# Attention weights and gates from sigmoids and a running product, in place of clamp, exp, ln, running sum and exp

## The chip, the cores and the metric

The kernel runs on one core of a Trainium2 chip. The metric is device time in microseconds (us). Three timed runs of the kernel before gave 1094.94, 1096.07 and 1101.93 us, so its time is 1096.07 us (median).

The engines of the core are named as the profile names them. PE is TensorE, which multiplies matrices, and PEld is its loading of weights. DVE is VectorE, ACT is ScalarE, POOL is GpSimd, and SP is SyncE, which issues transfers. Each engine works through its own queue in order and waits on semaphores for the others. Matmul results land in eight PSUM banks, numbered 0 to 7 here. In this kernel DVE and ACT read them, and POOL does not.

## The reference

The kernel is one layer of a streaming encoder over 1024 tokens of width 1024, all in float32. One input projection feeds three groups of heads (stick-breaking attention, an mLSTM matrix memory, a gated MLP). Then come one output projection, a mixture of 32 experts and a gated embedding. Three pieces of it matter here:

```python
# stick-breaking attention, 6 heads of 64, query blocks of 128 (n = 0..7), scale = 1/8
z = jnp.einsum('bthd,bshd->bhts', q[:, t0:kend], k[:, :kend]) * scale
mask = spos[None, :] < tpos[:, None]
log_1m = jnp.where(mask, -jax.nn.softplus(z), 0.0)
after = lax.cumsum(log_1m, axis=3, reverse=True) - log_1m
a = jnp.where(mask, jnp.exp(jax.nn.log_sigmoid(z) + after), 0.0)
outs.append(jnp.einsum('bhts,bshd->bthd', a, v[:, :kend]))
...
# mLSTM inputs: convolved queries and keys, and the log of the forget gate
qk = jax.nn.silu(causal_depthwise_conv(jnp.concatenate([qb, kb], axis=-1), conv_w[i], conv_b[i]))
bcum = jnp.cumsum(jax.nn.log_sigmoid(f_pre.reshape(Bn, N, L, H)), axis=2)
...
yb = hb * jax.nn.sigmoid(ob)
```

The weight of key s for query t is sigmoid(z_s) times the product, over the keys after s, of one minus their sigmoid. The reference forms that product as the exponential of a sum of logs.

## The kernel before, in words

The program has three parts in time. First the input is normed and turned, and the first columns of the input projection are made (up to about 87 us of the span). Then the rest of the input projection and the whole attention run interleaved (about 87 to 460 us). After that come the mLSTM rows, the output projection, routing, experts and the embedding. The change touches the second part alone.

**Steps and slots.** The attention is cut into 48 `Step`s: 6 heads times 8 query blocks, in the order of blocks (0, 7, 1, 6, 2, 5, 3, 4). A step of block i has 128 queries and n = 128 (i + 1) keys, so small and large steps alternate. The order in which every engine gets its work is written out by hand (L1077 to L1120): a loop over 58 slots (`NSLOT + 2`), and in slot s each stage of the pipeline is issued for another step. The second number below is how many slots after its scores a stage of the same step comes.

- `scores` (0): PE makes z into banks 3 and 4, at most 512 columns each, and adds a large negative number over the diagonal block's masked part.
- `clamp` (1): DVE reads z from PSUM, scales it by 1/8, caps it at 40 and writes `zc`. One instruction for each bank, 72 in all.
- `softplus` (1): ACT makes exp of `zc` into `sp`, then ln(1 + sp).
- `sums` (2): DVE makes the running sum of `sp` from the last key to the first, then POOL subtracts it from `zc`.
- `weights` (3): ACT makes exp of that.
- `turned` (4): PE transposes the weights into banks 5 and 6.
- `high` and `low` (5): ACT copies them to float16, and DVE makes the float16 remainder.
- `values` (6): PE multiplies with the values into bank 7, and `finish` (7): DVE adds the two halves into `ya`.

In a slot the queues of DVE, ACT and POOL receive `finish`, `clamp`, `high`, `weights`, `softplus`, `sums`, `low`, and then the side work. PE receives half a projection group, `values`, the rest of the slot's projection work, `turned`, `scores`. The 88 half groups of the projection are spread over 56 slots, so one or two fall into a slot, with shorter matmuls for some groups than for others.

**Side work.** What follows a projection is a generator that moves on by one stage for each slot. `ob_out` makes the output gate sigmoid(ob): DVE scales and caps, ACT does exp, ln(1 + .) and exp(-.), POOL multiplies with a gain. `conv_out` makes the causal convolution of 128 rows by 1024 tokens with four DVE instructions, then the SiLU in the same way: DVE caps (L548), ACT does exp, ln and exp, POOL multiplies. There are 8 `ob` tiles and 6 convolutions. `gate_rows` makes the mLSTM gates from exp and ln and, later, three exps. Other side work is the splitting of the next weights into two float16 parts (ACT L259, DVE L252), the gated MLP (`sgu`) and the splitting of the output weights (L140 and L141).

**Buffers.** `zc` has two buffers for each of two widths (512 and 1024), `sp` has one for each width. The weights for the experts are read into memory that the input projection uses, so their transfers can only be issued when this part is over.

**Activation tables.** ACT evaluates functions from a loaded table set, and a load is an instruction of its own, `ACT_TABLE_LOAD`. Before, the set with both exp and ln is loaded at the start (L149) and again after the one GELU (L480, L481). The experts begin with another (L1800).

Of the kernel before, what the change touches and what calls it, by code (L numbers as in the profile page):

```python
# [10 lines left out]
F32 = mybir.dt.float32  # L11
F16 = mybir.dt.float16
I32 = mybir.dt.int32
AF = mybir.ActivationFunctionType
# [29 lines left out]
ZCLAMP = 40.0  # L44
# [51 lines left out]
def hybrid_kernel(ctx, tc, x, p, norm1_g, w_in, conv_w, conv_b, igate_b, fgate_b, mnorm_g, sb_out_g,  # L96
# [52 lines left out]
    nc.scalar.preload_act_table_set("natural_log_exp_and_others")  # L149
# [28 lines left out]
    # DRAM scratch  # L178
# [12 lines left out]
    # one arena whose slices are first the operands of the input projection, then expert weights  # L191
# [13 lines left out]
    class Slots:  # L205
        """Slices of the arena in turn, by tag."""
# [15 lines left out]
    # matmuls whose results nothing reads: they keep the clock of the tensor engine up while it waits  # L222
# [72 lines left out]
    V = vp.tile([P, NT, HA, 2, DA], F16, name="V")  # L295

# [135 lines left out]
    # work that follows a projection moves on by one stage per slot  # L432
# [43 lines left out]
    def uv_out(pz, a, t):  # L476
        nc.scalar.activation(uv[:, t, a], pz[:, :WU], AF.Copy, scale=ISW)
        yield
        if a and t == NT - 1:
            nc.scalar.activation(uv, uv, AF.Gelu_apprx_tanh)  # L480
            nc.scalar.preload_act_table_set("natural_log_exp_and_others")  # L481
            side.append(sgu_all())
# [16 lines left out]
    def ob_out(pz, t):  # L499
        zr = wp.tile([P, HM * (DM + 1)], F32, "zr")[:, :WM]  # L500
        nc.vector.tensor_scalar(gates[:, :, t], pz[:, WM:WM + 8].rearrange("p (q h) -> p q h", q=2), ISW, None, op0=OP.mult)
        nc.vector.tensor_scalar(zr, pz[:, :WM], -ISW, ZCLAMP, op0=OP.mult, op1=OP.min)
        yield
        nc.scalar.activation(zr, zr, AF.Exp)
        nc.scalar.activation(zr, zr, AF.Ln, bias=one1)
        nc.scalar.activation(zr, zr, AF.Exp, scale=-1.0)
# [24 lines left out]
    def conv_out(pz, jj, half):  # L531
# [16 lines left out]
        nc.vector.tensor_scalar(sg, ca, -1.0, ZCLAMP, op0=OP.mult, op1=OP.min)  # L548
        yield
        nc.scalar.activation(sg, sg, AF.Exp)  # L550
        nc.scalar.activation(sg, sg, AF.Ln, bias=one1)
        nc.scalar.activation(sg, sg, AF.Exp, scale=-1.0)
# [10 lines left out]
    # gate rows: partition = (chunk of P tokens, head), column = token of the chunk  # L563
    def gate_rows():
# [18 lines left out]
        yield  # L583
        nc.scalar.activation(ga, ga, AF.Exp)
# [37 lines left out]
    # output projection weights, over what the attention no longer needs  # L622
# [13 lines left out]
    class Step:  # L636
# [18 lines left out]
        def clamp(self):  # L655
            self.w = 512 if self.n <= 512 else S
            self.zc = at.tile([P, self.w], F32, name=f"zc{self.h}{self.i}", tag=f"zc{self.w}")
            for s0, m, pz in self.z:
                nc.vector.tensor_scalar(self.zc[:, s0:s0 + m], pz[:, :m], 0.125, ZCLAMP, op0=OP.mult, op1=OP.min)  # L659

        def softplus(self):
            self.sp = at.tile([P, self.w], F32, name=f"sp{self.h}{self.i}", tag=f"sp{self.w}", bufs=1)
            nc.scalar.activation(self.sp[:, :self.n], self.zc[:, :self.n], AF.Exp)  # L663
            nc.scalar.activation(self.sp[:, :self.n], self.sp[:, :self.n], AF.Ln, bias=one1)

        def sums(self):
            n, sp = self.n, self.sp[:, :self.n]
            nc.vector.tensor_tensor_scan(sp[:, ::-1], one1.to_broadcast([P, n]), sp[:, ::-1],  # L668
                                         0.0, op0=OP.mult, op1=OP.add)
            nc.gpsimd.tensor_tensor(self.zc[:, :n], self.zc[:, :n], sp, op=OP.subtract)  # L670

        def weights(self):
            nc.scalar.activation(self.zc[:, :self.n], self.zc[:, :self.n], AF.Exp)

        def turned(self):
            h, i = self.h, self.i
            self.t = []
            for s0 in range(0, i + 1, 4):
                m = min(4, i + 1 - s0)
                pt = bank("56", f"at{h}{i}{s0}")  # L680
                for b in range(m):
                    nc.tensor.transpose(pt[:, b * P:(b + 1) * P], self.zc[:, (s0 + b) * P:(s0 + b + 1) * P], ident)
                self.t.append((m, pt))

        def high(self):
            self.a = []
            for s, (m, pt) in enumerate(self.t):
                ah = at.tile([P, 512], F16, name=f"ah{self.h}{self.i}{s}", tag="ah", bufs=3)
                nc.scalar.activation(ah[:, :m * P], pt[:, :m * P], AF.Copy)
                self.a.append(ah)  # L690

        def low(self):
            for s, (m, pt) in enumerate(self.t):
                al = at.tile([P, 512], F16, name=f"al{self.h}{self.i}{s}", tag="al", bufs=3)
                nc.vector.tensor_tensor(al[:, :m * P], pt[:, :m * P], self.a[s][:, :m * P], op=OP.subtract)
                self.a[s] = [(self.a[s][:, b * P:(b + 1) * P], al[:, b * P:(b + 1) * P]) for b in range(m)]

        def values(self):
            self.pa = bank("7", f"av{self.h}{self.i}")[:, :P].rearrange("p (l d) -> p l d", l=2)
            for sb, (ah, al) in enumerate(sum(self.a, [])):  # L700
# [21 lines left out]
    class Rows:  # L722
        """mLSTM chunk, output projection, second norm and routing of P tokens."""
# [165 lines left out]
        # the last tile goes to the router without the way over its rows in memory  # L889
# [97 lines left out]
        def slots(self, which="4"):  # L987
# [8 lines left out]
            # the tokens of the first two experts are also found without the way through memory  # L996
# [68 lines left out]
    with tc.manual_schedule(engines=FOUR):  # L1065
# [11 lines left out]
        for s in range(NSLOT + 2):  # L1077
# [24 lines left out]
            stage(s - 7, "finish")  # L1102
            stage(s - 1, "clamp")
            stage(s - 5, "high")
            stage(s - 3, "weights")
            stage(s - 1, "softplus")
            stage(s - 2, "sums")
            stage(s - 5, "low")
# [5 lines left out]
            stage(s - 6, "values")  # L1114
# [3 lines left out]
            stage(s - 4, "turned")  # L1118
# [29 lines left out]
    # the slot table: (token, row of h2 to add to, weight)  # L1148
# [27 lines left out]
    # LE[., t, e]: whether token t needs no expert after e  # L1176
# [760 lines left out]
```

## Time and profile before

| what | value |
|---|---|
| time, median of 3 runs | 1096.07 us (1094.94 to 1101.93) |
| span of the profiled execution | 1098.5 us |
| PE busy | 948.8 us (86%) |
| DVE busy | 785.3 us (71%) |
| ACT busy | 626.7 us (57%) |
| POOL busy | 433.0 us (39%) |

For the profiled execution the page lists its span and no other time, so its span is taken as its time; it lies inside the range of the timed runs. Shares are means over the whole span, and the three parts of the program have different limits, so the second part is best read by stretches. A row of the view by stretches gives the stretch, its length, and for each engine its busy microseconds with the number of instructions, then the granted PE clock (1.00 is full) and the share of the transfer engines. A row of a group of instructions gives line, engine, operation, what is written from what, shapes and count, then the busy time, the mean nanoseconds of one, and the idle time of the engine just before them with what ended it. In a timeline the idle time before an instruction stands in square brackets.

### The profile page before, as it was taken

To read this page: it belongs to the slowest core of one execution; us is meant where nothing else is said; L and a number is where in the kernel's file an instruction comes from. 1 tells how busy PE (TensorE), PEld (TensorE's weight loads), DVE (VectorE), ACT (ScalarE), POOL (GpSimd) and SP (SyncE) were. 2 spreads that over 40 slices of the span, in tenths; PEclk is the share of its full clock that TensorE was granted. 3 is DMA by queue.
4 is the path that set the end of the run, shared out by engine and by line. 5 is a ranking of instruction groups with operands and counts; after the bars stand their busy time and mean duration, and the time that the engine had idled before them with its cause. 6 is when DMAs were issued, how large, how long until landed. Compare 5 with 4: busy or idle time off the path is not lost. (4 is left out here: it accounts for less than half of the span.)

```text
span 1098.5 us, 16018 instructions
## 1 busy us (share of the span) xinstructions
PE 948.8 (86%) x5927; PEld 546.8 (50%) x5928; DVE 785.3 (71%) x1345; ACT 626.7 (57%) x960; POOL 433.0 (39%) x381
## 2 busy tenths in 40 slices
PE   7899988877899887899788569998899989999796
PEld 4458845444465454665554334444454544544343
DVE  4444659998896997657888747898668686776333
ACT  4335565555587665423343247898667777686422
POOL 2101215454344244322323636854346445552421
PEclk8999989999899988899998689999899999999998
DMA  6421112021221127885348688999979898997330
GB/s 213 124 50 28 36 48 53 20 68 60 70 90 37 35 76 235 254 264 173 102 135 269 207 272 266 318 305 309 301 248 309 259 327 280 291 316 254 76 87 38
DMA packets 128466, 189.55 MB, mean 173 GB/s; under 512 B 13505, under 2 KB 104223, under 8 KB 128384
## 3 DMA queue, kind: packets, MB, share of 16 engines
q1 hardware_dynamic: 113376, 154.40, 43.6%
q0 software_dynamic: 14864, 33.57, 11.2%
q8 instruction: 47, 0.77, 0.3%
q10 hardware_dynamic: 144, 0.52, 0.1%
q14 instruction: 35, 0.29, 0.1%
HBM read 166.01 MB, written 37.31 MB: 185 GB/s over the span
## 5 line engine op out<-in xcount | busy, mean ns | idle before, releaser
L670 POOL TENSOR_TENSOR zc<-zc,sp 128x128 f32<-128x128 f32 (+7 forms) x48 | 71.6, 1491 | 192.8 <-DVE sp L668 174.4
L1277 POOL DMA_INDIRECT h2s<-yo,tabs x32 | 75.7, 2366 | 75.7 <-issue 24.6
L144 PE MATMUL pg<-arena,xT 128*128 128x512 f16 x256 | 97.6, 381 | 0.9 <-ACT xT L1239 0.7
L145 PE MATMUL pg<-arena,xT 128*128 128x512 f16 x256 | 97.8, 382 | 0.0
L146 PE MATMUL pg<-arena,xT 128*128 128x512 f16 x256 | 97.8, 382 | 0.0
L141 DVE SCALAR_TENSOR_TENSOR arena<-arena 128x2048 f16<-128x2048 f32 (+1 forms) x39 | 80.9, 2088 | 22.6 <-ACT arena L140 22.6
L146 PEld LDWEIGHTS <-arena 128*128 128x128 f16 x516 | 52.3, 101 | 53.0 <-issue 12.0
L141 DVE SCALAR_TENSOR_TENSOR arena<-ws,arena 128x2048 f16<-128x2048 f32 x29 | 65.9, 2288 | 14.3 <-ACT arena L140 14.3
L144 PEld LDWEIGHTS <-arena 128*128 128x128 f16 x516 | 53.3, 103 | 38.6 <-issue 7.3
L145 PEld LDWEIGHTS <-arena 128*128 128x128 f16 x516 | 52.4, 102 | 38.7 <-issue 11.4
L140 ACT ACTIVATE arena<-arena 128x2048 f16<-128x2048 f32 (+1 forms) x39 | 67.1, 1738 | 3.8 <-DMA arena<-in_w_up_dram 3.8
L668 DVE TENSOR_TENSOR_SCAN sp<-one,sp 128x128 f32<-128x128 f32 (+7 forms) x48 | 68.1, 1418 | 0.3
L663 ACT ACTIVATE sp<-zc 128x128 f32<-128x128 f32 (+7 forms) x48 | 32.7, 681 | 57.7 <-DVE zc L659 57.5
L659 DVE TENSOR_SCALAR zc<-z 128x512 f32<-128x512 f32 (+3 forms) x72 | 37.5, 548 | 28.9 <-PE z L650 17.8
L140 ACT ACTIVATE arena<-ws 128x2048 f16<-128x2048 f32 x29 | 55.1, 1920 | 0.1
L145 PE MATMUL pd<-dl,hT 128*128 128x512 f16 x120 | 47.0, 392 | 5.4 <-DVE dl L141 5.3
L144 PE MATMUL po<-woh,yT 128*128 128x512 f16 x128 | 50.3, 393 | 0.0
L145 PE MATMUL po<-wol,yT 128*128 128x512 f16 x128 | 50.2, 392 | 0.0
L146 PE MATMUL po<-woh,yT 128*128 128x512 f16 x128 | 49.9, 390 | 0.0
L144 PE MATMUL pd<-dh,hT 128*128 128x512 f16 x120 | 47.2, 394 | 1.6 <-ACT yo L1274 1.5
L701 PE MATMUL av<-V,ah 128*128 128x128 f16 x216 | 25.7, 224 | 26.2 <-DVE ya L707 26.0
L141 DVE SCALAR_TENSOR_TENSOR dl<-arena,dh 128x2048 f16<-128x2048 f32 x17 | 38.9, 2288 | 11.7 <-ACT dh L140 11.7
(664 smaller groups left out, 2858.2 us busy)
## 6 DMA issues: line engine op xcount, KB each, us to landing
arena<-in_w_down_dram SPq DMA_DIRECT2D x19, 1024.0 KB, 11.8
arena<-in_w_up_dram SPq DMA_DIRECT2D x18, 1024.0 KB, 12.4
arena<-in_w_gate_dram SPq DMA_DIRECT2D x17, 1024.0 KB, 10.1
ws<-in_w_gate_dram SPq DMA_DIRECT2D x14, 1024.0 KB
ws<-in_w_up_dram SPq DMA_DIRECT2D x13, 1024.0 KB, 10.7
ws<-in_w_down_dram SPq DMA_DIRECT2D x12, 1024.0 KB, 5.6
arena<-in_w_in_dram SPq DMA_DIRECT2D x16, 384.0 KB, 7.2
x<-in_x_dram SPq DMA_DIRECT2D x8, 512.0 KB, 3.4
```

The lines of the kernel that those rows point to most:

```text
L140: nc.scalar.activation(hi, src, AF.Copy, scale=scale)
L141: nc.vector.scalar_tensor_tensor(lo, src, scale, hi, op0=OP.mult, op1=OP.subtract)
L144: nc.tensor.matmul(o, a[0], w[0], start=first, stop=False)
L145: nc.tensor.matmul(o, a[0], w[1], start=False, stop=False)
L146: nc.tensor.matmul(o, a[1], w[0], start=False, stop=last)
L659: nc.vector.tensor_scalar(self.zc[:, s0:s0 + m], pz[:, :m], 0.125, ZCLAMP, op0=OP.mult, op1=OP.min)
L663: nc.scalar.activation(self.sp[:, :self.n], self.zc[:, :self.n], AF.Exp)
L668: nc.vector.tensor_tensor_scan(sp[:, ::-1], one1.to_broadcast([P, n]), sp[:, ::-1], 0.0, op0=OP.mult, op1=OP.add)
L670: nc.gpsimd.tensor_tensor(self.zc[:, :n], self.zc[:, :n], sp, op=OP.subtract)
L701: nc.tensor.matmul(self.pa.rearrange("p l d -> p (l d)"), ah, V[:, sb, self.h].rearrange("p l d -> p (l d)"), start=(sb == 0), stop=False)
L1277: return nc.gpsimd.indirect_dma_start(out=h2s, out_offset=bass.IndirectOffsetOnAxis(ap=self.tb[:, 1:2], axis=0), in_=self.yo, in_offset=No ...
```

## The change: what it does

The weights of the attention are made as sigmoid(z/8) times the running product of sigmoid(-z/8) over the later keys, and the two gates as sigmoids. For the attention:

- `clamp` and `softplus` become `sigmoids` (1 slot after the scores, as before): ACT reads z from PSUM twice, once for sigmoid(-z/8) into `rest` and once for sigmoid(z/8) into `a`. With two banks these are four instructions, with one bank two.
- `sums` becomes `products` (2): DVE makes the running product of `rest` in place from the last key to the first, with the two operations of the scan both multiplications; POOL multiplies `a` with `rest` shifted by one column. A column of ones stands after the last key.
- `weights` is gone, and `turned`, `high`, `low`, `values` and `finish` each come one slot earlier.
- `rest` has one buffer for each width, as `sp` had; `a` has two, as `zc` had.

In `ob_out` one sigmoid of ACT from PSUM replaces DVE's capping and three ACT instructions, and the POOL multiplication comes one slot earlier. In `conv_out` one sigmoid replaces DVE's capping and three ACT instructions. The table set with the sigmoid is loaded at the start and after the GELU. `gate_rows` still needs exp and ln and loads the set with both in the middle of the attention; a function that the loaded set lacks gets a load in front of it.

```diff
-    nc.scalar.preload_act_table_set("natural_log_exp_and_others")
+    nc.scalar.preload_act_table_set("sigmoid_and_others")
...
     V = vp.tile([P, NT, HA, 2, DA], F16, name="V")
+
+    rests = {w: vp.tile([P, w + 1], F32, name=f"rest{w}") for w in (512, S)}
+    for w in rests:
+        nc.gpsimd.memset(rests[w][:, w:], 1.0)
...
             nc.scalar.activation(uv, uv, AF.Gelu_apprx_tanh)
-            nc.scalar.preload_act_table_set("natural_log_exp_and_others")
+            nc.scalar.preload_act_table_set("sigmoid_and_others")
...
-        nc.vector.tensor_scalar(zr, pz[:, :WM], -ISW, ZCLAMP, op0=OP.mult, op1=OP.min)
-        yield
-        nc.scalar.activation(zr, zr, AF.Exp)
-        nc.scalar.activation(zr, zr, AF.Ln, bias=one1)
-        nc.scalar.activation(zr, zr, AF.Exp, scale=-1.0)
+        nc.scalar.activation(zr, pz[:, :WM], AF.Sigmoid, scale=ISW)
         yield
...
-        nc.vector.tensor_scalar(sg, ca, -1.0, ZCLAMP, op0=OP.mult, op1=OP.min)
-        yield
-        nc.scalar.activation(sg, sg, AF.Exp)
-        nc.scalar.activation(sg, sg, AF.Ln, bias=one1)
-        nc.scalar.activation(sg, sg, AF.Exp, scale=-1.0)
+        yield
+        nc.scalar.activation(sg, ca, AF.Sigmoid)
         nc.gpsimd.tensor_tensor(ca, ca, sg, op=OP.mult)
...
+        nc.scalar.preload_act_table_set("natural_log_exp_and_others")
         nc.scalar.activation(ga, ga, AF.Exp)
         nc.scalar.activation(ga, ga, AF.Ln, bias=one1[:R])
...
-        def clamp(self):
+        def sigmoids(self):
             self.w = 512 if self.n <= 512 else S
-            self.zc = at.tile([P, self.w], F32, name=f"zc{self.h}{self.i}", tag=f"zc{self.w}")
+            self.rest = rests[self.w]
+            self.a = at.tile([P, self.w], F32, name=f"a{self.h}{self.i}", tag=f"a{self.w}")
+            o = self.w - self.n
             for s0, m, pz in self.z:
-                nc.vector.tensor_scalar(self.zc[:, s0:s0 + m], pz[:, :m], 0.125, ZCLAMP, op0=OP.mult, op1=OP.min)
-
-        def softplus(self):
-            self.sp = at.tile([P, self.w], F32, name=f"sp{self.h}{self.i}", tag=f"sp{self.w}", bufs=1)
-            nc.scalar.activation(self.sp[:, :self.n], self.zc[:, :self.n], AF.Exp)
-            nc.scalar.activation(self.sp[:, :self.n], self.sp[:, :self.n], AF.Ln, bias=one1)
-
-        def sums(self):
-            n, sp = self.n, self.sp[:, :self.n]
-            nc.vector.tensor_tensor_scan(sp[:, ::-1], one1.to_broadcast([P, n]), sp[:, ::-1],
-                                         0.0, op0=OP.mult, op1=OP.add)
-            nc.gpsimd.tensor_tensor(self.zc[:, :n], self.zc[:, :n], sp, op=OP.subtract)
-
-        def weights(self):
-            nc.scalar.activation(self.zc[:, :self.n], self.zc[:, :self.n], AF.Exp)
+                nc.scalar.activation(self.rest[:, o + s0:o + s0 + m], pz[:, :m], AF.Sigmoid, scale=-0.125)
+            for s0, m, pz in self.z:
+                nc.scalar.activation(self.a[:, s0:s0 + m], pz[:, :m], AF.Sigmoid, scale=0.125)
+
+        def products(self):
+            n, w = self.n, self.w
+            back = self.rest[:, w - n:w][:, ::-1]
+            nc.vector.tensor_tensor_scan(back, back, one1.to_broadcast([P, n]), 1.0, op0=OP.mult, op1=OP.mult)
+            nc.gpsimd.tensor_tensor(self.a[:, :n], self.a[:, :n], self.rest[:, w - n + 1:w + 1], op=OP.mult)
...
-            stage(s - 7, "finish")
-            stage(s - 1, "clamp")
-            stage(s - 5, "high")
-            stage(s - 3, "weights")
-            stage(s - 1, "softplus")
-            stage(s - 2, "sums")
-            stage(s - 5, "low")
+            stage(s - 6, "finish")
+            stage(s - 4, "high")
+            stage(s - 1, "sigmoids")
+            stage(s - 2, "products")
+            stage(s - 4, "low")
             advance()
...
-            stage(s - 6, "values")
+            stage(s - 5, "values")
...
-            stage(s - 4, "turned")
+            stage(s - 3, "turned")
             stage(s, "scores")
```

More of the change, by code (lines that the diff above doesn't have):

```diff
@@ L43 @@
 BIG = 1 << 20
-ZCLAMP = 40.0
 NB = WM + 8
@@ L681, in turned @@
                 for b in range(m):
-                    nc.tensor.transpose(pt[:, b * P:(b + 1) * P], self.zc[:, (s0 + b) * P:(s0 + b + 1) * P], ident)
+                    nc.tensor.transpose(pt[:, b * P:(b + 1) * P], self.a[:, (s0 + b) * P:(s0 + b + 1) * P], ident)
                 self.t.append((m, pt))
         def high(self):
-            self.a = []
+            self.hl = []
             for s, (m, pt) in enumerate(self.t):
@@ L689, in high @@
                 nc.scalar.activation(ah[:, :m * P], pt[:, :m * P], AF.Copy)
-                self.a.append(ah)
+                self.hl.append(ah)
         def low(self):
@@ L694, in low @@
                 al = at.tile([P, 512], F16, name=f"al{self.h}{self.i}{s}", tag="al", bufs=3)
-                nc.vector.tensor_tensor(al[:, :m * P], pt[:, :m * P], self.a[s][:, :m * P], op=OP.subtract)
-                self.a[s] = [(self.a[s][:, b * P:(b + 1) * P], al[:, b * P:(b + 1) * P]) for b in range(m)]
+                nc.vector.tensor_tensor(al[:, :m * P], pt[:, :m * P], self.hl[s][:, :m * P], op=OP.subtract)
+                self.hl[s] = [(self.hl[s][:, b * P:(b + 1) * P], al[:, b * P:(b + 1) * P]) for b in range(m)]
         def values(self):
             self.pa = bank("7", f"av{self.h}{self.i}")[:, :P].rearrange("p (l d) -> p l d", l=2)
-            for sb, (ah, al) in enumerate(sum(self.a, [])):
+            for sb, (ah, al) in enumerate(sum(self.hl, [])):
                 nc.tensor.matmul(self.pa.rearrange("p l d -> p (l d)"), ah,
```

## The prediction

> **What bounds the kernel now.** I read the page first. Its chain of what ended last names only the end of the program, so I go by the slices and then by stretches.
>
> ```profile
> DVE  4444659998896997657888747898668686776333
> PEclk8999989999899988899998689999899999999998
> ```
>
> Each digit is 27.5 us. DVE reads 9, 9, 9, 8, 8, 9, 6, 9, 9 from slice 7 on, which is 165 to 412 us, and the PE clock dips to 8 or 9 in the same place. That is the attention. The view by stretches, cut where the slots change character:
>
> ```profile
> core 0: us, PE busy (x) PEld busy (x) DVE busy (x) ACT busy (x) POOL busy (x), PEclk, DMA share, GB/s
> 87.00:147.00 60.00, 58.85 (x535) 48.93 (x534) 36.28 (x51) 37.27 (x67) 14.83 (x10) 1.00 0.16 43
> 147.00:319.00 172.00, 140.15 (x870) 80.51 (x868) 152.97 (x316) 102.95 (x176) 76.97 (x64) 0.92 0.19 54
> 319.00:365.00 46.00, 45.45 (x327) 27.45 (x325) 36.94 (x69) 34.00 (x61) 17.17 (x17) 1.00 0.14 44
> 365.00:402.00 37.00, 31.33 (x197) 17.30 (x196) 36.34 (x48) 25.02 (x43) 13.32 (x8) 0.91 0.20 61
> 402.00:462.00 60.00, 45.08 (x306) 30.68 (x305) 41.87 (x80) 29.87 (x66) 24.66 (x39) 0.89 0.71 213
> ```
>
> I call these A to E. In A and C PE is busy 98 and 99%: nothing that DVE or ACT saves there can move the end. In B DVE is busy 89% and PE 81%, in D 98 and 85%. Who keeps PE waiting in B:
>
> ```profile
> PE av L701 <- DVE ya L707: 17.4, 10, 3.6
> PE at L682 <- DVE al L695: 8.7, 6, 2.2
> ```
>
> These 26.1 us are most of PE's 31.85 us of idle time in B (172.00 less 140.15). `values` waits until DVE has emptied bank 7 with `finish`, and `turned` until DVE has emptied banks 5 and 6 with `low`. Both are short DVE instructions that stand late in a full queue. So DVE bounds B and D, and the change takes instructions from that queue.
>
> **What leaves DVE.** The capping of `clamp` (L659), in B and in D:
>
> ```profile
> 147.00:319.00 172.00, 17.02 (x33) 0.92 0.19 54
> 365.00:402.00 37.00, 3.77 (x7) 0.91 0.20 61
> ```
>
> That of the convolutions (L548):
>
> ```profile
> 147.00:319.00 172.00, 2.08 (x3) 0.92 0.19 54
> 365.00:402.00 37.00, 1.39 (x2) 0.91 0.20 61
> ```
>
> That of `ob_out` (L502), in B:
>
> ```profile
> 147.00:319.00 172.00, 1.90 (x4) 0.92 0.19 54
> ```
>
> B loses 17.02 + 2.08 + 1.90 = 21.00 us and keeps 131.97. D loses 3.77 + 1.39 = 5.16 and keeps 31.18.
>
> B: at the occupancy of now (152.97 / 172.00 = 0.889) 131.97 us of DVE work take 148.4 us, still above PE's 140.15. Gain 23.6. From below it is 0, if DVE's largest pieces set the waits and not its total. From above DVE cannot beat 131.97, a gain of 40.0. I take 23.6, because the waits on DVE are spread over 16 places and not over two or three.
>
> D: DVE's 31.18 at 0.982 gives 31.7, PE has 31.33. Gain 5.0, between 0 and 5.7.
>
> E holds the end of the last convolution and of the last steps. Two PE waits stand out:
>
> ```profile
> 406.95 0.22 PE L701 MATMUL av<-V,ah 128*128 128x128 f16 x1 [3.21 <-DVE ya L707]
> 416.95 0.22 PE L701 MATMUL av<-V,ah 128*128 128x128 f16 x1 [3.76 <-DVE ya L707]
> 413.52 2.58 DVE L141 SCALAR_TENSOR_TENSOR wol<-arena,woh 128x1024 f16<-128x1024 f32 x1 [3.65 <-ACT woh L140]
> ```
>
> The second arises because DVE waits 3.65 us for ACT's copy of the output weights, which stood in ACT's queue behind the last convolution's exp, ln and exp. Two of those three go. Of the 6.97 us I take 4.0, between 0 and 7.0.
>
> **What changes on ACT.** The three passes over each step, and what a PSUM read by ACT costs at each width:
>
> ```profile
> L663 ACT ACTIVATE sp<-zc 128x128 f32<-128x128 f32 (+7 forms) x48 | 32.7, 681 | 57.7 <-DVE zc L659 57.5
> L664 ACT ACTIVATE sp<-sp,one 128x128 f32<-128x128 f32 (+7 forms) x48 | 37.2, 775 | 1.6
> L673 ACT ACTIVATE zc<-zc 128x128 f32<-128x128 f32 (+7 forms) x48 | 32.7, 680 | 7.2 <-POOL zc L670 7.2
> L689 ACT ACTIVATE ah<-at 128x512 f16<-128x512 f32 x35 | 20.0, 591 | 14.4 <-PE at L682 14.3
> L689 ACT ACTIVATE ah<-at 128x384 f16<-128x384 f32 x12 | 5.8, 485 | 2.0 <-PE at L682 2.0
> L689 ACT ACTIVATE ah<-at 128x256 f16<-128x256 f32 x12 | 4.5, 378 | 2.2 <-PE at L682 2.2
> L689 ACT ACTIVATE ah<-at 128x128 f16<-128x128 f32 x11 | 2.9, 267 | 0.0
> ```
>
> Out go 32.7 + 37.2 + 32.7 = 102.6 us. In come two passes over 36 pieces of 512 columns and 12 each of 384, 256 and 128: 2 x (36 x 591 + 12 x (485 + 378 + 267)) ns = 69.7 us. The sigmoid is not in the trace; a copy from PSUM of the same size is the nearest row. ACT loses 32.9 us here and more in the gates, but it is busy at most 74% of a stretch (C), so I count no gain of its own. The 57.5 us for which exp waited on `clamp` become a wait on z itself, one engine fewer in between. What queues behind that wait is the second pass and ACT's side work, as now.
>
> Table loads are new. The loaded set changes in `gate_rows` to exp and ln, back for the next step, to exp for the three late exps, back, and to exp for the mLSTM rows: five more than now.
>
> ```profile
> 143.80 1.28 ACT L480 ACT_TABLE_LOAD   x1
> 145.09 3.62 ACT L480 ACTIVATE woh<-woh 128x4096 f32<-128x4096 f32 x1
> ```
>
> One takes 1.28 us and the next activation follows at once, so 6.4 us in all. Where they fall:
>
> ```profile
> 356.78 0.29 ACT L584 ACTIVATE gr<-gr 32x128 f32<-32x128 f32 x1
> 381.49 0.38 ACT L610 ACTIVATE gr<-gr 32x128 f32<-32x128 f32 x1
> ```
>
> The first pair comes in C, where ACT has 12.00 us idle, the second in D, where it has 11.98, the fifth in E. On the path I count 1.5, between 0 and 6.4.
>
> The Trainium skill, page "ScalarE: Activation LUTs", section "What ACT_TABLE_LOAD costs", agrees on the 1283 ns but adds about 1380 ns of drain for each switch, 2.66 us together. By it the five would be 13.3 us, an estimate, and the term at most that. The trace shows no such idle time after the load.
>
> **What stays the same.** The scan keeps its length, direction and two operations, and multiplies where it added. Two scans on the gates with other operations:
>
> ```profile
> L588 DVE TENSOR_TENSOR_SCAN gr<-gr 32x128 f32<-32x128 f32 x1 | 0.4, 412 | 0.0
> L589 DVE TENSOR_TENSOR_SCAN gr<-one,gr 32x128 f32<-32x128 f32 x1 | 0.4, 385 | 0.0
> ```
>
> They differ by 27 ns at equal length, 7%, so a product scan costs between 27 ns less and 27 ns more each, 48 x 27 = 1.3 us either way: 0. POOL multiplies where it subtracted; its multiplications by the gain show how far that may differ:
>
> ```profile
> L508 POOL TENSOR_TENSOR arena<-arena,gy 128x384 f32<-128x384 f32 x8 | 8.9, 1113 | 0.0
> L670 POOL TENSOR_TENSOR zc<-zc,sp 128x384 f32<-128x384 f32 x6 | 6.0, 1001 | 21.7 <-ACT sp L663 13.1 <-DVE sp L668 8.6
> ```
>
> At most 11% of POOL's time, and POOL is busy 77 of 172 us in B: 0. The two memsets of ones come before the attention, 0. No transfer is added; `zob` leaves a slot earlier. The slots remain 58, so dropping a stage shortens nothing by itself.
>
> **What the shorter pipeline costs.** Two waits lose slack. The scores of the next step need a bank that ACT now holds for up to three passes (3 x 591 ns) where DVE needed one; and `turned` now waits for the POOL product of the slot just before, where the exp on ACT and a whole slot lay between. Behind `turned` in PE's queue stand the next scores and the next projection. For the largest step the product ends one scan and one multiplication after DVE begins:
>
> ```profile
> L668 DVE TENSOR_TENSOR_SCAN sp<-one,sp 128x1024 f32<-128x1024 f32 x6 | 13.7, 2281 | 0.0
> L670 POOL TENSOR_TENSOR zc<-zc,sp 128x1024 f32<-128x1024 f32 x6 | 14.5, 2419 | 31.5 <-DVE sp L668 31.5
> L652 PE MATMUL z<-negm,identh x48: 219/219/314, 88.1 to 401.6; 128*128 128x128 f16 x48
> ```
>
> That is 4.7 us, against a mean slot of 313.5 / 47 = 6.7 us, so the cover holds on average; it fails where a short slot follows a full DVE queue. I count 2.0 us, between 0 and the 14 us of a rival below.
>
> **The sum.** 23.6 + 5.0 + 4.0 - 1.5 - 2.0 = 29.1 us. What follows begins with transfers that can only be issued when the projections are done, so it moves along whole. From the profiled span of 1098.5 us that gives 1069.4; the span is 2.4 us above the median of the runs, 1096.07, so I forecast 1067 us.
>
> **The rivals.**
>
> More (12%): PE's clock comes back in B. There it is granted 0.92, and 1.00 in A and C where PE hardly waits. Without the waits PE's 140.15 us would shrink towards 0.92 x 140.15 = 128.9, and B would come to DVE's 131.97: a gain of 40.0 in place of 23.6, so 1051. Against it: DVE would have to run without a gap. The Trainium skill, page "TensorE: Matmul & The Clock Gate", Part 1, gives a rule for that: about 3.4 us of idle PE halves the clock. It speaks for this rival, since the waits listed above reach 3.6.
>
> Less (17%): `turned` waits for POOL's product. If each of the 24 large steps, some 11 of them in B, costs 1.3 us (a 4.7 us chain against the 3.4 us that such a short slot leaves), 14 us are lost: 1081. For it speaks that POOL stretches when DVE is busy; against it that DVE becomes freer.
>
> None (10%): the waits on DVE come from its pieces of several us in a row, convolutions and weight splits, which stay. Then only E and part of D gain, about 8 us after the loads: 1088. Against it: 89 and 98% of DVE over whole stretches.
>
> Slower (5%): ACT must reload its table within the slot, because a copy or a square is not served by the sigmoid's set. Two loads for each of 48 steps are 96 x 1.28 = 123 us. If half of it stays hidden, 62 us come on the path: 1129. It decides from about 23 uncovered loads on (29.1 / 1.28). Against it: beside the two loads of the GELU there are only these, and copies and squares run under the sets of both:
>
> ```profile
> L149 ACT ACT_TABLE_LOAD x1 | 1.3, 1283 | 0.8 <-PEq L1923 0.8
> L1800 ACT ACT_TABLE_LOAD x1 | 1.3, 1283 | 0.0
> ```
>
> The forecast itself has 56%, with a range of its own of 1060 to 1076: up with all loads on the path (4.9) and nothing in E (4.0), down with the upper ends of D and E (3.7) and nothing lost to loads and slack (3.5).
>
> **How the numbers follow.** This kernel's runs agree to about 1%, 11 us, which is what a measurement can tell from no change: faster means below 1085. Forecast, More and Less lie there, 85%; None is within, 10%; 5% is slower. A range of 1046 to 1088 takes in More with the upper ends of D and E and no cost of loads (5.2 below 1051), Less, and the half of None below 1088; what it leaves out is the slower case, the other half of None and the far ends, some 15%.
>
> **What the profile after would show.** In the stretch that answers to B, DVE loses some 21 us of work and PE's waits for L707 and L695 fall from 26 us to under 10, with the clock above 0.92. A and C stay as long as they are, with PE at 97% or more. Five more table loads, each 1.28 us, none of them every slot. The sigmoid's passes take 591 ns at 512 columns. If PE instead waits in front of `turned` for POOL, Less is right; if waits of 3 us behind the convolutions remain, None is. The forecast is wrong if B is still above 160 us.

## The result, and the profile after

The kernel after takes 1064.49 us, the median of four runs (1063.04 to 1068.76), against 1096.63 us for the kernel before in four runs beside it (1094.94 to 1101.93). The ratio is 0.9696, with a 95% interval of 0.9664 to 0.9728: 32.1 us faster, where 29 were forecast. The profiled execution after took 1063.69 us, 0.8 us below the median, and has a span of 1061.8 us. Where a run lists both, its time is 1.5 to 2.9 us longer than its span, so the profiled execution before, with a span of 1098.5 us, lay some 3 to 5 us above its median, an estimate. The two traces therefore differ by 36.7 us and the medians by 32.1: the gains that are read from stretches below are together 4.6 us more than the timed gain.

The slices of the page after, as shown of before, one digit for 26.5 us:

```profile
DVE  4454549999957965578888649897677777686333
PEclk8999989999999997999988789999999999999898
```

DVE reads 9 in slices 7 to 11 and in slice 14, where it read 8 or 9 in eight slices, and the clock reads 9 from slice 7 to 15, where there were two 8s. The stretches A to E of the kernel after, cut at the ends of the same slots (busy us of each engine with the count of instructions, then clock and transfers):

```profile
core 0: us, PE busy (x) PEld busy (x) DVE busy (x) ACT busy (x) POOL busy (x), PEclk, DMA share, GB/s
87.70:146.30 58.60, 58.60 (x540) 48.97 (x539) 29.20 (x38) 30.85 (x70) 12.34 (x10) 1.00 0.17 44
146.30:292.70 146.40, 131.80 (x873) 77.87 (x871) 131.18 (x279) 76.10 (x164) 74.86 (x65) 0.95 0.22 65
292.70:338.00 45.30, 45.30 (x334) 27.74 (x332) 28.05 (x53) 25.12 (x54) 14.95 (x15) 1.00 0.13 41
338.00:368.90 30.90, 27.30 (x185) 15.60 (x186) 30.66 (x35) 19.44 (x41) 13.95 (x9) 1.00 0.25 89
368.90:428.20 59.30, 44.75 (x298) 30.29 (x296) 37.72 (x73) 26.05 (x61) 23.17 (x36) 0.85 0.72 207
```

At the exact slot ends the kernel before had 59.5, 172.2, 45.7, 37.1 and 60.2 us. The gains are therefore 0.9, 25.8, 0.4, 6.2 and 0.9 us, and 2.5 us lie outside the five. B carries 70% of the 36.7 us. DVE lost 21.8 us of work there (152.97 to 131.18), and B became 25.8 us shorter, while A and C, where PE is now busy without a gap, kept their length to within 1 us. What keeps PE waiting on DVE in B of the kernel after (us in total, times, the longest):

```profile
PE av L695 <- DVE ya L701: 10.7, 6, 3.8
PE at L676 <- DVE al L689: 2.1, 2, 1.8
```

The same two waits, `values` for `finish` and `turned` for `low`, made 26.1 us before and make 12.8 now. No wait of `turned` on POOL stands in A to D.

### The profile page after: what moved, and what is told of

It reads as the page before. It is cut to its first block, busy times and chain, and to the rows that moved or that the text cites. A ratio compares the mean times of both kernels' runs of the same rounds, so it can differ in the third digit from the quotient of the medians.

```text
span 1061.8 us, 15986 instructions
## 1 busy us (share of the span) xinstructions
PE 931.5 (88%) x5927; PEld 538.3 (51%) x5928; DVE 741.1 (70%) x1259; ACT 574.9 (54%) x937; POOL 425.5 (40%) x383
## 5 line engine op out<-in xcount | busy, mean ns | idle before, releaser
L667 POOL TENSOR_TENSOR a<-a,rest 128x128 f32<-128x128 f32 (+7 forms) x48 | 60.7, 1264 | 169.9 <-DVE rest L666 129.0
L1269 POOL DMA_INDIRECT h2s<-yo,tabs x32 | 72.0, 2251 | 72.2 <-issue 25.2
L666 DVE TENSOR_TENSOR_SCAN rest<-rest,one 128x128 f32<-128x128 f32 (+7 forms) x48 | 73.8, 1538 | 7.0 <-ACT rest L659 6.7
L145 PEld LDWEIGHTS <-arena 128*128 128x128 f16 x516 | 51.8, 100 | 50.2 <-DVE arena L251 6.5
L144 PEld LDWEIGHTS <-arena 128*128 128x128 f16 x516 | 51.7, 100 | 39.1 <-issue 10.9
L143 PEld LDWEIGHTS <-arena 128*128 128x128 f16 x516 | 52.3, 101 | 37.1 <-issue 4.9
L683 ACT ACTIVATE ah<-at 128x512 f16<-128x512 f32 (+3 forms) x72 | 32.6, 488 | 37.1 <-PE at L676 36.6
L143 PE MATMUL pd<-dh,hT 128*128 128x512 f16 x120 | 47.6, 397 | 3.4 <-ACT yo L1266 3.3
L689 DVE TENSOR_TENSOR al<-at,ah 128x512 f16<-128x512 f32 (+3 forms) x72 | 36.9, 540 | 17.9 <-ACT ah L683 17.9
L145 PE MATMUL pd<-dh,hT 128*128 128x512 f16 x120 | 47.3, 394 | 0.0
```

Of the source, the lines that this page charges most:

```text
L143: nc.tensor.matmul(o, a[0], w[0], start=first, stop=False)
L144: nc.tensor.matmul(o, a[0], w[1], start=False, stop=False)
L145: nc.tensor.matmul(o, a[1], w[0], start=False, stop=last)
L666: nc.vector.tensor_tensor_scan(back, back, one1.to_broadcast([P, n]), 1.0, op0=OP.mult, op1=OP.mult)
L667: nc.gpsimd.tensor_tensor(self.a[:, :n], self.a[:, :n], self.rest[:, w - n + 1:w + 1], op=OP.mult)
L689: nc.vector.tensor_tensor(al[:, :m * P], pt[:, :m * P], self.hl[s][:, :m * P], op=OP.subtract)
```

## The experiments

Each run was compared with the kernel before on the same chip; "against after" means the difference of the two ratios to it, times its 1100 us (medians of 1099.62 to 1099.86). A row of the view by stretches is that of B, cut at the same slot ends. My theory was that DVE's queue bounds B and D, so that what DVE no longer does there is the gain. The rivals were that ACT's shorter chain, or the dropped stage, is.

**DVE's capping put back.** In front of the sigmoids DVE makes a scaled and capped copy of z again. Nobody uses it.

```diff
+            for s0, m, pz in self.z:
+                nc.vector.tensor_scalar(junk[:, :m], pz[:, :m], 0.125, 40.0, op0=OP.mult, op1=OP.min)
             for s0, m, pz in self.z:
                 nc.scalar.activation(self.rest[:, o + s0:o + s0 + m], pz[:, :m], AF.Sigmoid, scale=-0.125)
```

> The changed kernel, but DVE again makes the capped copy of every bank of scores, at its old place in the queue, into a tile that nobody reads: DVE gets its 72 instructions back (37.5 us by the profile of before), ACT keeps two passes, the pipeline stays one stage shorter. Theory (DVE's full queue was the bound, so what left DVE made the gain): 17.0 us over an occupancy of 0.889 are 19 us in stretch B, 4 more in D, so about 1088 us, between 1082 and 1096; the PE waits for the emptying of banks 7 and 5/6 come back to over 20 us. Rival (the gain came from ACT's fewer passes or from the shorter pipeline): the time stays at 1064 to 1070.

Measured: 1081.39 us, ratio 0.9831 (0.9799 to 0.9864), 14.8 us against after.

```profile
149.50:306.40 156.90, 134.10 (x872) 77.33 (x870) 144.81 (x309) 75.65 (x161) 73.23 (x64) 0.96 0.20 60
```

With 13.6 us more of DVE, B is 10.5 us longer, and ACT's work is what it was. The direction is the theory's, but the size is less: the time lies just under its 1082 to 1096, and B grew by 10.5 us where 19 were expected. One thing is mixed in: the sigmoid had to wait for the copy in DVE's queue, as the exp had waited for `clamp`. In B of this kernel, with its own line numbers:

```profile
ACT rest L662 <- DVE junk L660: 52.6, 22, 7.0
PE av L698 <- DVE ya L704: 11.5, 7, 3.6
PE at L679 <- DVE al L692: 6.1, 7, 2.0
```

PE's two waits came back to 17.6 us, not to over 20. ACT's wait of 52.6 us does not show up again behind ACT: in B every wait of PE is on DVE, and DVE waited for ACT 5.3 us where it waited 9.9 in the kernel after. So the rows speak for DVE's time and against this wait, but no run gave DVE the work without the wait.

**DVE's capping taken from the kernel before.** ACT scales z in its place, uncapped; the rest is the kernel before.

```diff
-                nc.vector.tensor_scalar(self.zc[:, s0:s0 + m], pz[:, :m], 0.125, ZCLAMP, op0=OP.mult, op1=OP.min)
+                nc.scalar.activation(self.zc[:, s0:s0 + m], pz[:, :m], AF.Copy, scale=0.125)
```

> The kernel before, with one edit: the scaled copy of the scores is made by ACT (a copy with scale 1/8, without the cap at 40) in place of DVE. Exp, ln, running sum, exp and the old depth stay, and ACT has a fourth pass, some 35 us more. Theory (DVE's queue): the gain of the capping alone without any sigmoid, 19 us in B and 4 in D, so about 1073, between 1067 and 1083; ACT in B rises to about 120 us of 150 and does not bind. Rival (ACT's passes set the time): no gain or slower, 1096 to 1115.

Measured: 1080.83 us, ratio 0.9814 (0.9779 to 0.9849), 20 us below before.

```profile
146.70:306.10 159.40, 137.16 (x870) 78.29 (x869) 138.21 (x283) 114.33 (x207) 78.37 (x63) 0.93 0.20 58
```

Here ACT does more than in either kernel (114.33 us of 159.40), exp, ln and exp all stand, no stage is dropped, and still B is 12.8 us shorter (19 were expected). The exp no longer waits for DVE here, so this run does not part DVE's time from that wait either. Moving this one step off DVE is worth 15 to 20 us of the 32, whichever kernel it is tried in.

**A third pass on ACT.** Each step's `a` is copied onto itself after its sigmoid.

```diff
                 nc.scalar.activation(self.a[:, s0:s0 + m], pz[:, :m], AF.Sigmoid, scale=0.125)
+            nc.scalar.activation(self.a[:, :self.n], self.a[:, :self.n], AF.Copy)
```

> The changed kernel with a third pass of ACT over each step: a plain copy of the weights onto themselves after the second sigmoid, some 33 us more of ACT in the attention, as many passes as before the change. DVE is not touched. Theory (DVE's queue bounds; ACT in B is busy 76 of 146 us): 1064 to 1070. Rival (the part of the gain that giving DVE its capping back did not undo, some 15 us, came from ACT's third pass): 1075 to 1084.

Measured: 1064.44 us, ratio 0.97 (0.9646 to 0.9753), nothing against after.

```profile
145.70:292.20 146.50, 131.33 (x873) 77.74 (x871) 130.73 (x278) 91.11 (x186) 74.69 (x64) 0.95 0.21 64
```

ACT works 15 us more in B, and B is as long as it was to 0.1 us. Two such copies behind each gate's sigmoid, tried alone, gave the same answer:

> The changed kernel with two plain copies by ACT after each gate's sigmoid, 8 of 384 columns and 6 of 1024 twice, 20 us of ACT in all, so the gates load ACT as before; DVE is untouched. Theory: 1063 to 1069. Rival (lumps of 3 us in ACT's queue delay the float16 copies, and through them DVE and PE): 1070 to 1077.

Measured: 1063.75 us, ratio 0.9683 (0.9645 to 0.9721). As long as DVE's queue is as light as it is after the change, the passes saved on ACT are worth nothing. Beside a full DVE queue they were not tried alone.

**The stages as late as before.** Each stage behind `products` is issued one slot later again.

```diff
-            stage(s - 6, "finish")
-            stage(s - 4, "high")
+            stage(s - 7, "finish")
+            stage(s - 5, "high")
...
-            stage(s - 4, "low")
+            stage(s - 5, "low")
...
-            stage(s - 5, "values")
+            stage(s - 6, "values")
...
-            stage(s - 3, "turned")
+            stage(s - 4, "turned")
```

> The changed kernel with turned, high, low, values and finish each issued one slot later, as before the change; nothing else differs. Theory: depth does not matter, because slots are set by DVE and PE work and the slots stay 58: 1061 to 1068. Rival one (the shorter pipeline made part of the gain): 1072 or more. Rival two (turned waits for the POOL product of the slot just before, the cost that the prediction booked at 2 us and at most 14): 1050 to 1061, with the waits in front of the transposes gone.

Measured: 1065.59 us, ratio 0.9674 (0.9637 to 0.9711). With the same delays, and a pass of ACT over the weights in the slot that this frees:

> The changed kernel with the old depth and, at the old place of the last exp, a plain copy of the weights by ACT: ACT again waits in the middle of its queue for POOL's product, and the float16 copies, sigmoids and side work stand behind that wait. DVE keeps its lightened queue. Theory (neither ACT's passes nor its waits set the time): 1062 to 1070. Rival (this wait is what the 12 us are that the capping and the gates' caps leave over): 1073 to 1081.

Measured: 1066.87 us, ratio 0.9715 (0.9669 to 0.9761). The dropped stage neither gains nor costs anything that these runs resolve: both differences, 2.4 us less and 2.1 us more, lie inside the intervals.

**The gates' caps put back.** DVE caps in `ob_out` and `conv_out`, and the sigmoid (with scale -1) follows from its result, in `ob_out` a slot later.

```diff
-        nc.scalar.activation(zr, pz[:, :WM], AF.Sigmoid, scale=ISW)
+        nc.vector.tensor_scalar(zr, pz[:, :WM], -ISW, 40.0, op0=OP.mult, op1=OP.min)
+        yield
+        nc.scalar.activation(zr, zr, AF.Sigmoid, scale=-1.0)
...
+        nc.vector.tensor_scalar(sg, ca, -1.0, 40.0, op0=OP.mult, op1=OP.min)
         yield
-        nc.scalar.activation(sg, ca, AF.Sigmoid)
+        nc.scalar.activation(sg, sg, AF.Sigmoid, scale=-1.0)
```

> The changed kernel, but DVE still caps the inputs of both gates (8 output gate tiles and 6 convolutions, 8.5 us of DVE by the profile of before) and the one sigmoid of ACT follows a slot later, as the exps did. Theory (DVE's queue): 4.0 us in B and 1.4 in D come back, at an occupancy of 0.9 some 5 us, so about 1070, between 1066 and 1074. Rival (only the attention's own chain counts): 1062 to 1066.

Measured: 1070.95 us, ratio 0.9751 (0.97 to 0.9803), 6.0 us against after, although the intervals still overlap.

```profile
147.40:296.70 149.30, 131.28 (x872) 77.40 (x871) 134.28 (x285) 75.94 (x163) 74.94 (x63) 0.95 0.21 62
```

DVE has 3.1 us more in B, and B is 2.9 us longer: the gates' caps fit the same account, DVE's time, as the attention's.

**All of the work put back at once.** Both DVE copies, the gates' two copies on ACT, the late stages and the pass over the weights together. Only the functions and the first pass's source are still those of the change.

> The changed kernel with all that it took away put back as work without effect: DVE's capped copy of the scores into a tile that nobody reads, DVE's caps in both gates, two plain copies by ACT after each gate's sigmoid, a plain copy of the weights by ACT after the POOL product at the old place of the last exp, and the old depth of the pipeline. Only the functions differ from the kernel before, and five table loads are more. Singly, the capping cost 15 us, the gates' caps 6, depth 0, a third ACT pass 0: together 21 of the 33. Theory (the rest comes from the pieces meeting in DVE's queue): 1092 to 1100, the whole gain gone. Rival (the sigmoid, the product scan or another thing that is not in this list gives the rest): 1083 to 1089.

Measured: 1096.35 us, ratio 0.9979 (0.9954 to 1.0004) in ten runs; the whole gain is gone. B and D:

```profile
147.50:316.20 168.70, 138.19 (x872) 80.27 (x870) 152.06 (x317) 98.95 (x198) 71.44 (x64) 0.93 0.18 55
362.10:400.90 38.80, 31.26 (x198) 17.17 (x197) 37.41 (x48) 26.63 (x48) 12.30 (x8) 0.91 0.22 72
```

and PE's waits in B, by the line numbers of that kernel, where L714 is `finish` and L702 is `low`:

```profile
PE av L708 <- DVE ya L714: 16.7, 8, 3.4
PE at L689 <- DVE al L702: 8.6, 6, 2.2
```

DVE's work, the clock and these waits (25.3 us) are about those of before; B is 3.5 us shorter than it was there and D 1.7 us longer. So the sigmoid as a function, and the product scan in place of the sum, give nothing by themselves beyond the 5 us that the interval leaves open. But tried singly the parts put back 14.8, 6.0, 0 and 0 us, some 21, and all at once 31. Which of them makes the other 10 us was not tried: the capping and the gates' caps were never put back together without the rest, so ACT's passes may count when DVE's queue is full.

**A table load for every step.** A load of another set and one of the sigmoid's set stand in front of each step's sigmoids, 96 in all.

```diff
+            nc.scalar.preload_act_table_set("exp_and_others")
+            nc.scalar.preload_act_table_set("sigmoid_and_others")
             for s0, m, pz in self.z:
```

> The changed kernel with two extra table loads in front of the sigmoids of every step, 96 of 1.28 us, 123 us of ACT in all. The prediction's slower rival counted half of it on the path. Theory (ACT has 70 us idle of 146 in B and 20 of 45 in C, but the loads stand in front of the sigmoids that free the banks for the next scores): A and C, where PE is busy all the time, begin to wait for ACT in the short slots; 1075 to 1100. Rival one (all hidden): 1064 to 1070. Rival two (half or more on the path): 1126 or more.

Measured: 1081.95 us, ratio 0.9874 (0.9806 to 0.9942), 19.6 us against after. The groups of its loads, and a wait of PE between 87 and 300 us that the kernel after lacks:

```profile
L658 ACT ACT_TABLE_LOAD x48 | 61.6, 1283 | 0.9
L659 ACT ACT_TABLE_LOAD x48 | 61.6, 1283 | 0.3
...
PE z L645 <- ACT a L663: 6.0, 8, 2.5
```

Of 123 us on ACT some 20 come on the path, 0.2 us for each load on average. A, B and C became 4.3, 5.8 and 3.5 us longer, and in them PE waited 8.8 us with the next scores for a bank that ACT had not read yet; the rest was not traced.

**More taken from DVE: the values' normalisation on ACT.** ACT makes (v - mean) times r as one activation with scale and bias, and in the first form the first tap of the convolutions too.

```diff
+        nb = u2.tile([P, NG], F32, name=f"nb{i}", tag="nb")
+        nc.vector.scalar_tensor_tensor(nb, mv[:, :, 0], -1.0, r, op0=OP.mult, op1=OP.mult)
...
-            nc.vector.tensor_scalar(vn[:, g], vt[:, g], mv[:, g, 0:1], r[:, g:g + 1], op0=OP.subtract, op1=OP.mult)
+            nc.scalar.activation(vn[:, g], vt[:, g], AF.Identity, scale=r[:, g:g + 1], bias=nb[:, g:g + 1])
...
-        nc.vector.tensor_scalar(ca, cx_[:, 3:], cw(3), vec[:, 40 + jj:41 + jj], op0=OP.mult, op1=OP.add)
+        nc.scalar.activation(ca, cx_[:, 3:], AF.Identity, scale=cw(3), bias=vec[:, 40 + jj:41 + jj])
```

> The changed kernel with two further pieces moved from DVE to ACT: the centring and scaling of the gated MLP's rows (32 instructions of 64 columns, some 21 us on DVE in the profile of before, most of it in B) and the first tap of the six convolutions (6.3 us). Results stay the same up to rounding. Theory (DVE still bounds B, 131.2 of 146.2 us busy, and ACT has 70 us idle there): B falls to what PE needs, 131.6 us and less at full clock, 8 to 13 us, so about 1053, between 1049 and 1060. Rival (PE or the order of the slots already bounds B): 1062 to 1067. Rival (ACT's queue matters): slower than 1066.

Measured: 1072.14 us, ratio 0.9727 (0.9686 to 0.9768): no gain over after, rather a loss. B, and in it the longest waits of ACT and of PE:

```profile
147.30:301.90 154.60, 133.60 (x872) 78.64 (x870) 119.86 (x252) 89.42 (x199) 71.47 (x65) 0.94 0.21 61
...
ACT arena L459 <- DVE nb L457: 31.5, 8, 5.2
PE av L697 <- DVE ya L703: 16.5, 6, 4.0
```

DVE had 11.3 us less to do, and B grew by 8.2 us. The moved step waits for `nb`, which DVE makes late in the same slot, and ACT stands still in front of it for up to 5.2 us while `high` and the sigmoids queue behind. DVE in turn waited 6.3 us in B for the moved tap; what each of the two pieces cost was not separated. The same move without the tap, and with ACT's part a slot later:

> The changed kernel with the centring and scaling of the gated MLP's rows on ACT (32 instructions, 21 us less on DVE), but one slot later than in the run where this and the first tap went to ACT and B became 8 us longer. There ACT waited 31.5 us in 8 places for a small DVE result that itself waits for POOL, with the float16 copies and sigmoids queued behind it. Now that result is ready a slot ahead. Theory (DVE's time bounds B as long as no queue waits in its place): B falls from 146 to 138 or less, 1053 to 1060. Rival (PE and the order of the slots bound B already, DVE's total no longer matters): 1062 to 1068.

Measured: 1061.24 us, ratio 0.9654 (0.9599 to 0.9708), the same as after within the intervals.

```profile
145.90:293.10 147.20, 133.51 (x872) 79.02 (x871) 125.59 (x254) 85.66 (x195) 75.35 (x64) 0.94 0.21 64
...
PE av L698 <- DVE ya L704: 4.7, 2, 3.8
PE pm L468 <- DVE nb L456: 2.5, 2, 1.4
```

PE's waits for `finish` fell from 10.7 to 4.7 us with DVE's work, yet B did not shorten: PE is busy 91% of it, and its waits came back in other places. They are 13.5 us in all, as the rows of the view add up, against 14.7 in the kernel after, and all are on DVE, some of them on the added `nb`. So B no longer follows how much DVE has to do. Whether PE bounds it, or the places at which DVE's short steps stand, the run does not tell.

**The output weights' copy on POOL.** On top of the last kernel POOL, not ACT, makes the high part of the output weights, in order to free ACT in E.

> The kernel with the gated MLP's rows normed on ACT one slot later, and with the high part of the output weights made by POOL in place of ACT. In E PE waits 8.4 us for ACT's emptying of projection banks, which stands in ACT's queue behind a copy of output weights that waits 2.8 us for its transfer; predicted gain in E was 4.0, measured 0.9. Theory (that wait on a transfer, seen through ACT, is what took the gain in E): E falls from 59 to 53 to 56, the time to 1055 to 1060. Rival (E is bound by the transfers of the output weights themselves or by the mLSTM rows' chain): E stays at 58 to 60, 1060 to 1066.

Measured: 1074.22 us, ratio 0.9774 (0.9733 to 0.9816), slower. The copy and its successor on DVE:

```profile
L633 POOL TENSOR_SCALAR woh<-arena 128x1024 f16<-128x1024 f32 x8 | 22.2, 2777 | 0.0
...
DVE wol L634 <- POOL woh L633: 28.3, 8, 6.1
```

POOL takes 2777 ns where ACT takes 1.06 us (in a row of E below), and DVE waits for it. This put a larger wait in E, so the run does not answer what holds E.

## Why the prediction was right, point by point

**How near the sum came.** That 32.1 us lie so close to 29.1 is partly luck, for the misses cancel. By the traces B, D, A and C and what lies outside gained 7.2 us more than their terms, and E 3.1 less; the 3.5 us taken off for loads and slack stand in no term, since what they cost is inside the stretches. And the trace of before is a long one, by the 3 to 5 us above.

**DVE bounds B and D: right.** The step from DVE's work to B's length, at equal occupancy, came near: 131.18 of 146.40 us is 0.896, against 0.889 before, and 23.6 forecast stand against 25.8. D gained 6.2 us, more than the 5.7 called its upper end, and than 5.3, which is what 37.00 less 31.7 gives in place of the 5.0 in the sum. That upper end took PE's 31.33 us as fixed, and they were not. In the run where ACT scales the scores, 198 instructions of PE in D took 28.63 us at a clock of 1.00, where 199 had taken 31.43 at 0.91. In the kernel after PE needs 27.30 us, also because 14 fewer of them fall into D, and DVE's 30.66 set the end.

The equal occupancy is not a law, though. Over the runs in which B is shown above, DVE's share of it went from 0.78 (the first move of the normalisation) to 0.92, and the same rule gave 19 us for the capping alone, where 10.5 and 12.8 were measured. Nor is DVE's busy time the amount of its work. The 32 normalisation steps of the gated MLP, which the change leaves as they are, took 20.7 us of B before, 14.6 after and 19.3 with the late stages. There DVE was busy 136.32 us, 5.1 more than after, and B was only 1.4 us longer:

```profile
145.80:293.60 147.80, 131.22 (x871) 76.52 (x869) 136.32 (x278) 75.62 (x163) 73.88 (x64) 0.97 0.21 64
```

The account is not additive either. DVE's capping alone took B to an occupancy of 0.923 (144.81 of 156.90), so its 13.6 us of work cost 10.5; all together, with 20.9 us more of DVE, cost B 22.3. What absorbs the first microseconds was not separated. One candidate is PE itself, whose work in B takes 131.80 us after and 138.19 with all put back, at clocks of 0.95 and 0.93, but this is argued and not shown.

**Waits in B under 10 us: missed.** They are 12.8. The longest, 3.8 us, comes right behind the GELU; the kernel before has it in the same place with 3.6 us. The prediction's "under 10" left no room for waits that the change does not touch.

**E: mis-sized.** I gave it 4.0 us and it gained 0.9. The step that failed is that the waits for `finish` would come off the path. They did go, from 7.0 to 2.5 us, but PE now stands elsewhere: for `low` 2.7 us in place of 0.5, and at `pvb` 4.1 in place of 2.4, while `pS` has 4.3 as it had 4.4. PE's waits in E after:

```profile
PE pS L775 <- ACT arena L519: 4.3, 2, 2.4
PE pvb L143 <- ACT arena L519: 4.1, 1, 4.1
PE at L676 <- DVE al L689: 2.7, 1, 2.7
PE av L695 <- DVE ya L701: 2.5, 2, 1.4
```

and ACT's queue in front of the second, with the idle time before an instruction in brackets:

```profile
396.96 1.06 ACT L139 ACTIVATE woh<-arena 128x1024 f16<-128x1024 f32 x1 [2.76 <-DMA arena<-in_w_out_dram]
...
398.80 0.48 ACT L519 ACTIVATE arena<-pvb 128x384 f32<-128x384 f32 x1
```

ACT's reading of a projection result stood behind an output weight whose transfer had not landed. E is also uneven. In the kernel with the gates' copies, which adds work on ACT and alters nothing else, it took 56.5 us:

```profile
368.60:425.10 56.50, 43.34 (x301) 29.69 (x299) 36.38 (x73) 28.32 (x63) 20.73 (x37) 0.91 0.73 217
```

So the gain lies between 0.9 and 3.7 in these traces. That the transfer is what holds E was not shown; the cause stays open.

**The five table loads: right, the price a little high.** Exactly five are new:

```profile
L659 ACT ACT_TABLE_LOAD x2 | 2.6, 1283 | 0.2
L580 ACT ACT_TABLE_LOAD x1 | 1.3, 1283 | 0.0
L607 ACT ACT_TABLE_LOAD x1 | 1.3, 1283 | 0.0
L769 ACT ACT_TABLE_LOAD x1 | 1.3, 1283 | 0.1
```

At the 0.2 us that the 96 loads cost each they make about 1 us on the path, an estimate, where I took 1.5. The Trainium skill, page "ScalarE: Activation LUTs", section "What ACT_TABLE_LOAD costs", adds some 1380 ns of drain for each switch. The rows agree with its 1283 ns and do not show the drain: the 96 loads of the experiment had 1.2 us of idle time before them in all, and behind a load the next activation begins at once, as here in the kernel after:

```profile
327.60 1.28 ACT L659 ACT_TABLE_LOAD   x1
328.89 0.28 ACT L659 ACTIVATE rest<-z 128x128 f32<-128x128 f32 x1
```

**The sigmoid passes: right.** Forecast were 69.7 us, from copies of 591 ns at 512 columns. By their means the 144 passes took 72 x (508 + 492) ns = 72.0 us (66.4 busy, since the records of passes that follow each other overlap), and 599 and 611 ns at 512:

```profile
L661 ACT ACTIVATE a<-z 128x512 f32<-128x512 f32 (+3 forms) x72 | 33.4, 508 | 0.0
L659 ACT ACTIVATE rest<-z 128x512 f32<-128x512 f32 (+3 forms) x72 | 33.0, 492 | 2.8 <-POOL a L667 1.3 <-PE z L649 0.6 <-PE z L647 0.4
L661 ACT ACTIVATE a<-z 128x512 f32<-128x512 f32 x36 | 21.2, 611 | 0.0
L659 ACT ACTIVATE rest<-z 128x512 f32<-128x512 f32 x36 | 21.0, 599 | 2.7 <-POOL a L667 1.3 <-PE z L649 0.6 <-PE z L647 0.4
```

The third pass showed that ACT's time weighs nothing in the kernel after.

**The shorter pipeline: 2.0 us not seen.** No wait of `turned` on POOL appears in A to D, and the late stages changed nothing beyond the intervals.

**The rivals.** Less needed that wait, and falls with it. None needed waits of some 3 us behind the convolutions; of `finish`'s waits in B only the one behind the GELU passes 3 us, and B lost 25.8. Slower needed loads in every step; when they were put there they cost 20 us and not 62, so even then the kernel would have stayed faster. Half of More is there: the clock came back from 0.92 to 0.95 in B and to 1.00 in D, and PE's busy time in B fell by 8.4 us for the same work. But B ended at 146.4 and not at DVE's 131.97, for DVE still has gaps. The Trainium skill, page "TensorE: Matmul & The Clock Gate", Part 1, ties the clock to PE's idle time, and the rows agree: where the waits went the clock rose, and in E, where they only changed their cause, it stayed low (0.89 before, 0.85 after).

## What to carry to other kernels

Divide the work of the engine that is full in a stretch by its occupancy there, take the moved instructions out, and hold the result against the next engine's busy time: here that gave the gain of B to within 10%, while for the capping alone it gave 19 us against 10.5 and 12.8. So take it as a first guess that can be almost twice too large. What was saved on an engine with spare time gave nothing as long as the full engine had been relieved. Take the next engine's busy time at full clock as its lower bound, since the clock can return with the waits: in D it did, from 0.91 to 1.00, in B to 0.95. Moving still more off the same engine stopped paying here when PE and DVE were about equally full, at 0.90 of B each, and a moved step must have its inputs ready a slot ahead, or it blocks the in-order queue that it moved to.

## What the runs showed that I had not expected

Some scans on DVE were stretched beside a two-input multiplication on POOL. From the timeline of the kernel after:

```profile
249.85 2.42 DVE L666 TENSOR_TENSOR_SCAN rest<-rest,one 128x128 f32<-128x128 f32 x1
249.64 2.35 POOL L549 TENSOR_TENSOR ca<-ca,cs 128x1024 f32<-128x1024 f32 x1
```

The six scans of 128 columns, as a group before and after:

```profile
L668 DVE TENSOR_TENSOR_SCAN sp<-one,sp 128x128 f32<-128x128 f32 x6 | 2.5, 415 | 0.1
L666 DVE TENSOR_TENSOR_SCAN rest<-rest,one 128x128 f32<-128x128 f32 x6 | 4.5, 747 | 0.6 <-ACT rest L659 0.6
```

The scan took 2.42 us where the mean before is 0.415, and it ended 0.28 us after POOL did. It began after POOL's multiplication. A scan of 896 columns that began 0.75 us before one, at 209.50 us, kept its 2.02 us, and POOL took 3.43 us there. In all the 48 scans take 73.8 us after and took 68.1 before, so the term "0, within 1.3 us" was low by 5.7. The operation is not the reason: with the capping put back the same product scans took 68.0 us, and in the kernel before with ACT scaling the scores the sum scans took 75.3. What changes, as far as the timeline shows, is when a scan meets POOL.

POOL's multiplication is cheaper than its subtraction was, beyond the 11% allowed for: 48 take 60.7 us where 71.6 were taken. This one goes with the operation, for with all the work put back the multiplications took 60.5 us, and the subtractions 70.1 with ACT scaling the scores.

```profile
L667 POOL TENSOR_TENSOR a<-a,rest 128x128 f32<-128x128 f32 (+7 forms) x48 | 60.7, 1264 | 169.9 <-DVE rest L666 129.0
```

And a table load's 1.28 us of ACT was worth only 0.2 us on the path on average, in a kernel where ACT had idle time to put it in.
